# Pinning every product of the tensor engine in the order in which it is written, in a two-layer decoder trunk

## The chip, the cores and the metric

The kernel runs on one core of one Trainium2 chip, as one program and one launch. Its time is the device time of one execution in microseconds (us). A profiled execution gives the trace that is read below; its span runs from the first to the last instruction.

## The reference

The trunk has two layers over 256 tokens of 1024 features, all in float32. A layer normalises the stream, multiplies it with one wide matrix `w_in`, feeds the pieces to a gated short convolution and to a four-head retention, merges both with sigmoid gates, projects, and adds; then comes a squared-ReLU MLP of width 4096:

```python
def hybrid_layer(x, positions, ...):
    h = rmsnorm(x, norm_mix)
    proj = h @ w_in
    cb, cc, cu, q, k, v, g, ga, gb = jnp.split(proj, split_points, axis=-1)
    y_conv = short_conv_mixer(cb, cc, cu, conv_w, w_conv_out)
    y_ret = retention_mixer(q, k, v, g, positions, ret_norm, w_ret_out)
    merged = jax.nn.sigmoid(ga) * y_conv + jax.nn.sigmoid(gb) * y_ret
    x = x + merged @ w_o
    h2 = rmsnorm(x, norm_mlp)
    return x + jnp.square(jax.nn.relu(h2 @ w_up)) @ w_down
```

After the second layer a last RMSNorm is applied.

## The kernel before

**Data.** Features lie on the 128 partitions, in eight feature tiles k = 0 to 7, and tokens along the free dimension. The weights come in blocks of 1 MB (1024 inputs by 256 outputs), 152 in all, each loaded by one DMA into a `raw` tile (the first three in pieces). A float32 number is represented by two reduced-precision parts: ScalarE (ACT) rounds it to the high part (L99), VectorE (DVE) subtracts to get the low part (L100). This `split` is done to every weight block, in two halves, into a `parts` tile, and to every activation that is to be multiplied. There are three `raw` and three `parts` buffers.

**A block's products.** `proj` (L159) multiplies one block with an activation: for each of the eight feature tiles and both halves of the outputs one product of 512 columns (high weights with both activation parts) and one of 256 columns (low weights with the high part), so 32 products per block, all through the helper `mm` (L156, L157), all adding into one `ps` tile. Four products belong to each feature tile. There are three `ps` buffers, so up to three projections can be open at once. `collect` (L206) then copies one half of the tile on ACT and adds the other on DVE. The first `v` block of layer 0 is multiplied unsplit.

**Stages.** In each layer: four `v` blocks; the convolution's `cc`, `cu`, `cb`; `q`, `k`, `g`, `ga`, `gb`, with the retention's products set in between by `later`; then four blocks with `yc` (the convolution's output), four with `yr` (the retention's), four with `mg` (the merge), sixteen up blocks on `mlp` (the second norm's input) and sixteen down blocks on `up0` to `up3`. The merged tiles 2p and 2p+1 of `mg` are made by a chain behind the p-th `yr` block: copy, add, gate, add, split. The tiles of `mlp` are made behind the p-th `mg` block: two adds into the stream `x` (L578), then a scaling on ACT (L246) and its low part on DVE (L247). The next layer's norm input `mix` is made in the same way behind the down blocks (L614, L246, L247). The last two feature tiles of layer 1's down projection go through `proj_one`, which adds the residual by two products with an identity matrix.

**Norms.** The factor of a norm is applied after the products, so it may come late. Squares are taken on ACT (L254), added on GpSimd (POOL, L258) and folded (L267), split into `mix_sh` and `mix_sl` (or `mlp_sh`, `mlp_sl`), and summed over the partitions by two products with a matrix of ones, `column_sums` (L229), into `mix_st` (`mlp_st`). `later(n, ...)` writes such a piece behind the n-th block from there: layer 0's first sums are written behind the third `v` block.

**What sets the order.** The kernel is built with a scheduler that lays out each engine's instructions by its own model of times. It may exchange instructions on one engine where no data forbids it. An instruction that is handed to `tc.keep_in_program_order` keeps its place in the written order among those that are handed to it. Before, that holds for the first product of each column sum (L231) and for the first squares. Once built, every engine's order is fixed.

Of the kernel before, what the change touches and what calls it, by code (L numbers as in the profile page):

```python
# [48 lines left out]
def trunk_kernel(ctx, tc, px, pos, w, cst, mask, out):  # L49
    nc = tc.nc  # L50
# [19 lines left out]
    ones = const.tile([P, P], F32R, name="ones")  # L70
# [7 lines left out]
    def stile(name):  # L78
        return s8.tile([P, KT, T], F32, tag="s8", name=name)
# [50 lines left out]
    def whole_tokens(xs):  # L130

        ps = ps_main.tile([P, 2, 2, T], F32, tag="mm", name="ps")
        raw = next_block()
        for k in range(KT):
            for j in range(2):
                mm(ps[:, j, 0], xs[:, k, j * P:(j + 1) * P], raw[:, 2 * k:2 * k + 2, :], k == 0, k == KT - 1)
        run_waiting()
        t = t2("sum", "sum", 4)
        nc.scalar.copy(t, ps[:, :, 0, :])
        return t  # L140
# [13 lines left out]
            due[0][1](*due[0][2])  # L154

    def mm(o, a, b, start, stop):  # L156
        nc.tensor.matmul(o, lhsT=a, rhs=b, start=start, stop=stop, skip_group_check=True)  # L157

    def proj(act, n_blocks=1):  # L159

        ps = ps_main.tile([P, 2, 2, T], F32, tag="mm", name="ps")
        for b in range(n_blocks):
            blk = next_block()
            for k in range(KT):
                a = act[b].at(k)
                for j in range(2):
                    first, end = b == 0 and k == 0, b == n_blocks - 1 and k == KT - 1  # L170
                    mm(ps[:, j], blk[:, 0, 2 * k + j, :], a, first, False)
                    mm(ps[:, j, 1], blk[:, 1, 2 * k + j, :], a[:, 0], False, end)
            run_waiting()
        return ps
# [53 lines left out]

    def column_sums(o, hi, lo):  # L229

        tc.keep_in_program_order(nc.tensor.matmul(o, lhsT=ones, rhs=hi, start=True, stop=False))  # L231
        nc.tensor.matmul(o, lhsT=ones, rhs=lo, start=False, stop=True)

    class Norm:

# [35 lines left out]
        def total(self):  # L271

            st = ps_misc.tile([P, T], F32, tag="misc", name=f"{self.name}_st")
            column_sums(st, *self.sums)
            return st
# [80 lines left out]
    for layer in range(DEPTH):  # L356
# [125 lines left out]
        def head_sums(i):  # L482

            st = ps_misc.tile([P, 2, T], F32, tag="misc", name="var_ps")
            h = slice(2 * i, 2 * i + 2)
            column_sums(st, osq[:, 0, h, :], osq[:, 1, h, :])
            nc.vector.tensor_scalar(
                out=rm[:, 1, h, :], in0=st, scalar1=1.0 / T, scalar2=EPS, op0=ALU.mult, op1=ALU.add
            )
            nc.scalar.activation(rm[:, 0, h, :], st, AF.Sqrt, scale=1.0 / T, bias=eps)  # L490
# [130 lines left out]
    o = stile("o")  # L621
# [35 lines left out]
    m, r, a = (small.tile([P, 2], F32, tag=n, name=n) for n in ("fin_m", "fin_r", "fin_a"))  # L657
# [95 lines left out]
```

## Time and profile before

| | us |
|---|---|
| median of 3 runs | 891.73 |
| lowest, highest | 891.69, 893.56 |
| the profiled execution | 892.27 |
| its span | 890.1 |
| PE busy in it | 877.3 |
| DVE busy in it | 695.9 |
| ACT busy in it | 505.4 |
| POOL busy in it | 251.7 |

The profile gives for each engine when an instruction started, how long it took, and what ended the idle time before it. PE is TensorE; PEld is its loading of weights, which overlaps its products. The ends of products are modelled, so a product's own duration is longer than the distance to the next one: distances between starts are the better measure. The granted clock of TensorE over the span is 0.994 of full speed.

### The profile page before, as it was taken

What the parts mean: (1) busy time and instruction counts of PE and PEld (TensorE: products, weight loads), DVE (VectorE), ACT (ScalarE), POOL (GpSimd) and SP (SyncE); (2) the same over time, 40 slices, a digit from 0 to 9 for tenths busy, and PEclk for the clock granted to TensorE, in tenths of its full rate; (3) what the DMA queues carried; (4) which work ended last, traced back from release to release, by engine and by line L of the source; (5) the groups of instructions that cost most, each with busy time, mean ns of one, the idle gap of its engine ahead of it and who ended that gap; (6) DMA issues with size and microseconds to landing.
All of it is one profiled execution on the core that took longest, in us unless ns stands there. A gap on an engine that the chain in (4) does not pass through costs nothing.

```text
span 890.1 us, 12685 instructions
## 1 busy us (share of the span) xinstructions
PE 877.3 (99%) x5090; PEld 767.9 (86%) x5090; DVE 695.9 (78%) x785; ACT 505.4 (57%) x700; POOL 251.7 (28%) x170
## 2 busy tenths in 40 slices
PE   8999999999999999999999999999999999999996
PEld 6878888888888888888888888888888888888896
DVE  5989999799977966555588989998996897664451
ACT  6445636675556877444455554566654597764440
POOL 2883353421003322000046324443200323210110
PEclk9999999999999999999999999999999999999998
DMA  9645645444654655555545553555355555555521
GB/s 319 233 141 190 205 159 199 179 159 148 231 188 143 237 193 188 192 192 188 193 179 190 189 190 142 189 190 177 130 215 189 189 180 206 189 200 190 191 75 48
DMA packets 24682, 163.00 MB, mean 183 GB/s; under 512 B 2864, under 2 KB 3504, under 8 KB 5552
## 3 DMA queue, kind: packets, MB, share of 16 engines
q1 hardware_dynamic: 24336, 161.68, 51.3%
q8 instruction: 40, 0.66, 0.3%
q10 hardware_dynamic: 288, 0.52, 0.2%
q14 instruction: 18, 0.15, 0.0%
HBM read 161.14 MB, written 1.05 MB: 182 GB/s over the span
## 4 chain that ended last, share of the span: by engine, by line
PE 92%; POOL 3%; DVE 2%; DMA 1%; ACT 1%; issue 0%; SPq 0%; DVEq 0%; POOLq 0%; ACTq 0%
PE ps L157 89%; PE o_ps L157 1%; DVE parts L100 1%; POOL sum L412 1%; DMA raw<-w 1%; PE sc_ps L157 1%; DMA px_sb<-px 0%; ACT parts L99 0%; POOL v L412 0%; POOL mix_sum L258 0%; POOL red L333 0%; POOL sum L432 0%; DVE o L675 0%; POOL turns L339 0%; DVE rs_a L215 0%
## 5 line engine op out<-in xcount | busy, mean ns | idle before, releaser
L100 DVE TENSOR_TENSOR parts<-raw,parts 128x1024 fp32r<-128x1024 f32 (+1 forms) x304 | 411.2, 1384 | 70.4 <-ACT parts L99 69.5
L99 ACT CAST parts<-raw 128x1024 fp32r<-128x1024 f32 (+1 forms) x304 | 302.4, 1044 | 109.2 <-PE ps L157 78.1
L157 PE MATMUL ps<-mix,parts 128*128 128x512 f32 (+1 forms) x1792 | 323.0, 341 | 2.5 <-DVE parts L100 2.5
L157 PEld LDWEIGHTS ps<-mix,parts 128*128 128x128 f32 x1792 | 275.9, 189 | 44.0 <-DVE parts L100 2.8
L157 PE MATMUL ps<-up,parts 128*128 128x512 f32 (+1 forms) x1088 | 179.4, 326 | 0.0
L157 PE MATMUL ps<-mlp,parts 128*128 128x256 f32 (+1 forms) x1024 | 178.5, 335 | 0.0
L157 PEld LDWEIGHTS ps<-up,parts 128*128 128x128 f32 x1088 | 159.1, 188 | 19.6
L157 PEld LDWEIGHTS ps<-mlp,parts 128*128 128x128 f32 x1024 | 155.4, 188 | 22.4 <-issue 0.4
L210 DVE TENSOR_TENSOR sum<-ps,sum 128x512 f32<-128x512 f32 x87 | 59.4, 683 | 43.7 <-ACT sum L209 43.7
L209 ACT COPY sum<-ps 128x512 f32<-128x512 f32 x87 | 50.6, 582 | 75.2 <-PE ps L157 75.2
L594 POOL TENSOR_TENSOR u<-u,rr2m 128x512 f32<-128x512 f32 x32 | 47.7, 1492 | 123.4 <-ACT u L604 106.1
L258 POOL TENSOR_TENSOR mix_sum<-mix_sum,sq 128x512 f32<-128x512 f32 x8 | 12.6, 1574 | 145.1 <-ACT sq L254 145.1
L258 POOL TENSOR_TENSOR mlp_sum<-mlp_sum,sq 128x512 f32<-128x512 f32 x6 | 12.9, 2158 | 122.7 <-ACT sq L254 122.7
L157 PE MATMUL ps<-yr,parts 128*128 128x512 f32 (+1 forms) x256 | 44.7, 336 | 0.0
L157 PE MATMUL ps<-mg,parts 128*128 128x512 f32 (+1 forms) x256 | 44.7, 336 | 0.0
L157 PE MATMUL ps<-yc,parts 128*128 128x512 f32 (+1 forms) x256 | 44.7, 336 | 0.0
L157 PEld LDWEIGHTS ps<-yc,parts 128*128 128x128 f32 x256 | 39.1, 188 | 5.2
L157 PEld LDWEIGHTS ps<-yr,parts 128*128 128x128 f32 x256 | 39.1, 188 | 5.2
L157 PEld LDWEIGHTS ps<-mg,parts 128*128 128x128 f32 x256 | 39.1, 188 | 5.2
L157 PE MATMUL ps<-parts,mix 128*128 128x512 f32 (+1 forms) x224 | 39.8, 338 | 0.0
L157 PEld LDWEIGHTS ps<-parts,mix 128*128 128x128 f32 x224 | 34.2, 188 | 5.0
L100 DVE TENSOR_TENSOR up<-u,up 128x512 fp32r<-128x512 f32 x32 | 26.1, 820 | 0.0
(175 smaller groups left out, 666.6 us busy)
## 6 DMA issues: line engine op xcount, KB each, us to landing
raw<-w SPq DMA_DIRECT2D x149, 1024.0 KB, 4.8
raw<-w SPq DMA_DIRECT2D x3, 512.0 KB, 7.5
raw<-w SPq DMA_DIRECT2D x5, 256.0 KB, 6.1
px_sb<-px SPq DMA_DIRECT2D x3, 256.0 KB, 4.6
mask_sb<-mask SPq DMA_DIRECT2D x1, 512.0 KB, 7.2
out<-o SPq DMA_DIRECT2D x2, 256.0 KB, 2.3
out<-o ACTq DMA_DIRECT2D x2, 256.0 KB, 2.5
raw<-w SPq DMA_DIRECT2D x2, 128.0 KB, 2.7
```

Of the source, the lines that this page charges most:

```text
L99: nc.scalar.copy(hi, src)
L100: nc.vector.tensor_tensor(out=lo, in0=src, in1=hi.bitcast(F32), op=ALU.subtract)
L157: nc.tensor.matmul(o, lhsT=a, rhs=b, start=start, stop=stop, skip_group_check=True)
L209: nc.scalar.copy(t, ps[:, :, 1, :])
L210: nc.vector.tensor_tensor(out=t, in0=ps[:, :, 0, :], in1=t, op=ALU.add)
L258: nc.gpsimd.tensor_tensor(out=self.sum, in0=self.sum, in1=sq, op=ALU.add)
L412: nc.gpsimd.tensor_scalar(out=o_, in0=t[:, c, :], scalar1=mu[:, c:c + 1], scalar2=None, op0=ALU.subtract)
L594: nc.gpsimd.tensor_tensor(out=u, in0=u, in1=both(rr2), op=ALU.mult)
```

## The change

`mm` hands its product to `tc.keep_in_program_order`, and `column_sums` goes through `mm`. So all products of the layers keep the order in which the source writes them; the six warm-up products, the sums of the last norm and its broadcast do not go through `mm`.

```diff
     def mm(o, a, b, start, stop):
-        nc.tensor.matmul(o, lhsT=a, rhs=b, start=start, stop=stop, skip_group_check=True)
+        tc.keep_in_program_order(nc.tensor.matmul(o, lhsT=a, rhs=b, start=start, stop=stop, skip_group_check=True))
...
     def column_sums(o, hi, lo):
 
-        tc.keep_in_program_order(nc.tensor.matmul(o, lhsT=ones, rhs=hi, start=True, stop=False))
-        nc.tensor.matmul(o, lhsT=ones, rhs=lo, start=False, stop=True)
+        mm(o, ones, hi, True, False)
+        mm(o, ones, lo, False, True)
```

On PE at the start of layer 0, - being the order before and + the order now (`ps_268`, `ps_335` and `ps_409` are the third, fourth and fifth block's results, `mix0_st` the first norm's column sums):

```order
 L157 MATMUL ps_268<-parts_108,mix01_103 128x512
 L157 MATMUL ps_268<-parts_108,mix01_103 128x256
+L157 MATMUL mix0_st_308<-mix0_sh_254,ones_91 128x256
+L157 MATMUL mix0_st_308<-mix0_sl_255,ones_91 128x256
 L157 MATMUL ps_335<-parts_215,mix00_102 128x512
 L157 MATMUL ps_335<-parts_215,mix00_102 128x256
...
-L231 MATMUL mix0_st_308<-mix0_sh_254,ones_91 128x256
...
-L232 MATMUL mix0_st_308<-mix0_sl_255,ones_91 128x256
```

Both sums moved from inside the fifth block to a place in front of the fourth. The orders of POOL, ACT and DVE up to the instruction that writes `mix0_sl` are the same in both; behind it DVE's Newton steps for the norm's factor moved forward, in front of the splits of the seventh block.

On PE at the first `mg` block of layer 0 (`ps_2239` and `ps_2286` are the first and second `mg` projection, `mg0` holds feature tiles 0 to 3 and `mg1` tiles 4 to 7):

```order
 L157 MATMUL ps_2239<-mg0_2042,parts_2142 128x512
 L157 MATMUL ps_2239<-mg0_2042,parts_2142 128x256
-L157 MATMUL ps_2286<-mg0_2042,parts_2190 128x512
-L157 MATMUL ps_2286<-mg0_2042,parts_2190 128x256
...
+L157 MATMUL ps_2239<-mg1_2043,parts_2142 128x512
+L157 MATMUL ps_2239<-mg1_2043,parts_2142 128x256
```

Before, the first projection's 16 products on `mg0` were followed by 6 of the second, then came 8 on `mg1` (tiles 4 and 5), 10 and 8 of the second, 6 of the third, and only then the first's last 8 (tiles 6 and 7): 54 products stood in front of them. Now 24 do. At `mlp` three projections' 48 products on tiles 0 to 3 stood in front of the first on tiles 4 and 5; now 16 do, and the column sums stand behind the second block instead of the middle of the third. At layer 1's first block 35 stood in front of tile 6; now 24 do. Layer 1's `mg` and `mlp` have the same exchange. In the tail the two identity products stand behind 48 products of their projection, without ten of the next one in front of or between them.

On DVE between `mg` and `mlp` of layer 0, before (`px_sb` holds the stream, `mlp00` feature tiles 0 to 3 and `mlp01` tiles 4 to 7 of the norm's input):

```order
L578 SCALAR_TENSOR_TENSOR px_sb_88<-ps_2335,px_sb_88 128x512
L578 SCALAR_TENSOR_TENSOR px_sb_88<-ps_2384,px_sb_88 128x512
L100 TENSOR_TENSOR parts_2443<-raw_2442,parts_2443 128x1024 x2
L578 SCALAR_TENSOR_TENSOR px_sb_88<-ps_2384,px_sb_88 128x512
L247 SCALAR_TENSOR_TENSOR mlp01_2238<-px_sb_88,mlp01_2238 128x256 x4
L100 TENSOR_TENSOR mlp0_sl_2435<-mlp0_sum_2236,mlp0_sh_2434 128x256
```

and now:

```order
L578 SCALAR_TENSOR_TENSOR px_sb_88<-ps_2335,px_sb_88 128x512 x2
L100 TENSOR_TENSOR parts_2386<-raw_2385,parts_2386 128x1024 x2
L247 SCALAR_TENSOR_TENSOR mlp01_2238<-px_sb_88,mlp01_2238 128x256 x2
L578 SCALAR_TENSOR_TENSOR px_sb_88<-ps_2384,px_sb_88 128x512 x2
L100 TENSOR_TENSOR parts_2443<-raw_2442,parts_2443 128x1024 x2
L247 SCALAR_TENSOR_TENSOR mlp01_2238<-px_sb_88,mlp01_2238 128x256 x2
L100 TENSOR_TENSOR mlp0_sl_2435<-mlp0_sum_2236,mlp0_sh_2434 128x256
```

The adds of each `mg` projection now stand together, followed by one block's splits and that projection's two feature tiles, which is the sequence that the down projections have before and after. The order of the DMA queue is the same.

## Rows read from the trace of the kernel before

**Rows 1.** The page's first part: busy us, share of the span, instructions.
```profile
PE 877.3 (99%) x5090; PEld 767.9 (86%) x5090; DVE 695.9 (78%) x785; ACT 505.4 (57%) x700; POOL 251.7 (28%) x170
```

**Rows 2.** PE's waits, longest first: total us, times, longest us.
```profile
PE ps L157 <- DVE parts L100: 2.5, 1, 2.5
PE ps L157 <- DMA raw<-w: 1.2, 2, 0.9
```

**Rows 3.** The chain that ended last: start us, us, what.
```profile
64.78 2.21 DVE parts L100
67.04 63.75 PE ps L157 x351
...
150.08 5.65 PE ps L157 x32
...
714.61 154.39 PE ps L157 x924
```

**Rows 4.** Stretches around 67 us: length, busy us, PEclk, DMA share, GB/s.
```profile
31.55:67.00 35.45, 33.03 (x188) 28.40 (x186) 32.32 (x45) 16.47 (x23) 30.78 (x26) 1.00 0.51 178
64.58:67.04 2.46, 0.01 (x2) 0.01 (x1) 2.46 (x3) 0.00 (x0) 1.32 (x1) 1.00 0.00 0
67.04:70.50 3.46, 3.46 (x11) 2.98 (x12) 2.77 (x4) 1.75 (x3) 0.00 (x0) 0.51 0.37 107
70.50:74.00 3.50, 3.50 (x22) 3.03 (x21) 3.36 (x3) 2.00 (x4) 2.37 (x1) 1.00 0.48 201
```

**Rows 5.** PE in order of time, 13 to 33 us: start us, us, instruction.
```profile
13.22 17.00 PE L157 MATMUL ps<-parts,mix 128*128 128x512 f32 x96
30.06 1.08 PE L157 MATMUL ps<-mix,parts 128*128 128x512 f32 x5
...
32.27 0.28 PE L232 MATMUL mix_st<-mix_sl,ones 128*128 128x256 f32 x1
```

**Rows 6.** POOL in order of time, 26 to 30 us.
```profile
26.96 1.30 POOL L258 TENSOR_TENSOR mix_sum<-mix_sum,sq 128x512 f32<-128x512 f32 x1
28.34 1.60 POOL L267 TENSOR_TENSOR mix_sum<-mix_sum 128x256 f32<-128x256 f32 x1
```

**Rows 7.** DVE in order of time, 23 to 32 us.
```profile
23.03 2.35 DVE L100 TENSOR_TENSOR parts<-raw,parts 128x1024 fp32r<-128x1024 f32 x2
...
31.55 0.41 DVE L100 TENSOR_TENSOR mix_sl<-mix_sum,mix_sh 128x256 fp32r<-128x256 f32 x1
```

**Rows 8.** PE in order of time, the `mg` stage of layer 0 and of layer 1.
```profile
244.88 22.35 PE L157 MATMUL ps<-mg,parts 128*128 128x512 f32 x128
...
678.00 22.35 PE L157 MATMUL ps<-mg,parts 128*128 128x512 f32 x128
```

**Rows 9.** DVE, the last split of `mg` in layer 0 and in layer 1.
```profile
249.90 0.68 DVE L100 TENSOR_TENSOR mg<-m,mg 128x512 fp32r<-128x512 f32 x1
...
683.03 0.68 DVE L100 TENSOR_TENSOR mg<-m,mg 128x512 fp32r<-128x512 f32 x1
```

**Rows 10.** DVE at the start of layer 1.
```profile
448.75 2.39 DVE L247 SCALAR_TENSOR_TENSOR mix<-px_sb,mix 128x256 fp32r<-128x256 f32 x2
451.33 0.43 DVE L100 TENSOR_TENSOR mix_sl<-mix_sum,mix_sh 128x256 fp32r<-128x256 f32 x1 [0.19 <-ACT mix_sh L99]
```

**Rows 11.** PE at the start of layer 1.
```profile
444.95 11.33 PE L157 MATMUL ps<-parts,mix 128*128 128x512 f32 x64
456.12 0.28 PE L231 MATMUL mix_st<-mix_sh,ones 128*128 128x256 f32 x1
```

**Rows 12.** POOL at the start of layer 1.
```profile
448.62 1.36 POOL L258 TENSOR_TENSOR mix_sum<-mix_sum,sq 128x512 f32<-128x512 f32 x1 [20.82 <-ACT sq L254]
```

**Rows 13.** Line L247: count, shortest, median and longest ns, first and last start.
```profile
L247 DVE SCALAR_TENSOR_TENSOR mlp<-px_sb,mlp x16: 470/476/1519, 262.9 to 707.2; 128x256 fp32r<-128x256 f32 x16
```

**Rows 14.** PE in the tail, the first identity product.
```profile
862.36 0.28 PE L157 MATMUL ps<-x_parts,ident 128*128 128x256 f32 x1
```

**Rows 15.** DVE in the tail, the identity product's operand.
```profile
859.82 1.52 DVE L100 TENSOR_TENSOR x_parts<-px_sb,x_parts 128x256 fp32r<-128x256 f32 x1
```

## The prediction

> **What bounds the kernel now.** I read the busy times first: TensorE (PE) is busy 99% of the span, VectorE (DVE) 78% [rows 1]. A busy share alone does not say which engine is the bound, so PE's own waits come next, longest first: one of 2.46 us on a DVE split of a weight block, and two on the first loads, 1.2 us together [rows 2]. The chain of waits says the same: from 67.04 us to 869 us it is PE products, one stretch behind the other [rows 3]. In there PE waits for nothing, so whatever idle time the change puts in is added to the end. Before 67 us there is the one wait to be won, and what follows it: in the 3.46 us behind it the granted clock is 0.51 of full speed, that is the lower of the two levels (1.2 instead of 2.4 GHz), and it is full again afterwards [rows 4]. That costs 3.46 x 0.49 = 1.7 us more.
>
> **What the change does.** It adds and removes no instruction, and the order of the DMA queue stays as it was. On PE it moves products at seven places: the first norm's two column sums, `yr` to `mg` and `mg` to `mlp` in each layer (the `mlp` column sums among them), the down projection to layer 1's first blocks, and the identity products of the tail. At each of them the scheduler had put products of the next `ps` tiles in front of products whose operand is late. A pinned product waits instead, and all that is queued behind it on PE waits too. So for each place I compare when the operand is ready with when PE, without gaps, would come to it.
>
> *The first column sums.* Before, they stand inside the fifth block's products, the second one at 32.27 us [rows 5]. Pinned, they stand in front of the fourth block. 96 products take from 13.22 to 30.06 us, 0.1754 us each [rows 5], so the 64 of the second and third block end at 13.22 + 64 x 0.1754 = 24.45 us. What the sums read is late for reasons that the change does not touch: POOL's third add of squares is queued behind two subtractions that wait for the second block's mean, and runs from 26.96 us, and the fold from 28.34 to 29.94 us [rows 6]; ACT then rounds it, and DVE writes the low part from 31.55 to 31.96 us [rows 7]. The rows of POOL, ACT and DVE up to there stand in the same order in the changed kernel. With 0.05 us to be seen by PE (a split that ended at 64.78 + 2.21 = 66.99 let PE go on at 67.04 [rows 3]) and 0.12 us for the second sum (256 columns, a third of the 768 of two products at 0.35 us), the fourth block starts at 32.12 instead of 24.45 us: **+7.67 us**. The two sums' 2 x 0.12 us inside the fifth block are gone: **-0.23**.
>
> *The wait at 64.58 us.* DVE is 32.3 us busy between 31.55 and 67.00 [rows 4], and that work ends with the block that PE waits for. PE now comes to that block 7.4 us later, at about 72 us, so DVE has some 40 us for 32.3 us of work, and the Newton steps for the norm's factor now stand in front of the seventh block's splits, in time that PE leaves open. The wait goes: **-2.46 us**. Should every DVE step move back with PE's releases, it stays; that is the other end, 0. The slow clock behind it goes too (-1.7), but PE stands idle three times as long at 24.45 us, and I charge the same 1.7 us there (bounds 0 and 3.4, twice the one stretch that the trace shows). Net nothing.
>
> *`yr` to `mg`, twice.* PE's `mg` products begin at 244.88 us [rows 8]. The first pinned projection wants feature tile 6 after 24 products, each 0.1765 us (5.65 us for 32 in the chain [rows 3]): 244.88 + 24 x 0.1765 = 249.12 us. The DVE operation that writes tiles 6 and 7 runs from 249.90 to 250.58 us, at the end of a row of operations that keeps its order [rows 9]. Plus 0.05: PE waits 1.51 us. Before, these products came 54 places behind the start, at 254.4 us, and waited for nothing. In layer 1 the same two rows lie 5.71 us apart (678.00 to 683.71) against 5.70 here [rows 8, 9], so **+3.0 us** for two. One DVE operation of that row, 0.7 us, earlier or later in each is the uncertainty: 1.6 to 4.4.
>
> *`mg` to `mlp`, twice, and down to layer 1's `mix`, once.* The third shows its price already. DVE reads the last down block in two adds, splits a weight block, and then writes feature tiles 6 and 7 of the norm's input, which end at 448.75 + 2.39 = 451.14 us [rows 10]. PE begins layer 1's products at 444.95 us [rows 11] and, pinned, wants tile 7 after 28 products, at 449.89. It waits 451.19 - 449.89 = 1.30 us in all, in two pieces, since tile 6 is late too. At `mlp` DVE and ACT now have the same sequence (two adds, a block's splits, two splits of the norm's input), where before the adds of several projections came in a bunch; I take 1.30 for each. The lower end is 0: the two last splits took 2.39 us with POOL adding squares beside them [rows 12]; at their shortest, 0.47 us each [rows 13], they end at 449.7, in time. **+3.9 us** for three.
>
> *Nothing.* The tail's identity products now come 48 instead of 54 products behind that block's start. The first is at 862.36 us before [rows 14], six products of 0.118 us earlier is 861.65; its operand is ready at 859.82 + 1.52 = 861.34 us [rows 15]. Layer 1's column sums wait for nothing either: their low part is there at 451.76, their place at 456.12 us [rows 10, 11], and `mlp`'s now have that place too.
>
> **Sum:** 7.67 - 0.23 - 2.46 + 3.0 + 3.9 = +11.9 us on the profiled execution's 892.27 us (span 890.1 and 2.2 around it), which is 904.2. The median of the runs is 0.54 us below that execution: 903.6 us.
>
> **The rivals.**
> *The clock falls at the short waits too.* The trace has a fall after 2.46 us of idling [rows 4] and none at the start after 0.9 us [rows 2]; 1.3 to 1.5 us lie between. Each fall would cost 1.7 us, five of them 8.5: 905.3 to 912.1 us. Against it: all five are nearer to the 0.9 than to the 2.46, and three come in two pieces. The Trainium skill ("TensorE: Matmul & The Clock Gate", section "A second HAM failure mode: psum-queue depth-cycling") tells of a kernel whose short idle times between groups of products made the clock swing between its levels; by that rule the sum would be the 912. No row here shows it for a wait of this length.
> *DVE does not catch up:* the 2.46 us wait and its slow clock come back, 903.6 + 4.2 = 907.8 us. For it: DVE is the fullest engine beside PE in that stretch, and the convolution's chain through POOL stands in front of the split. Against it: about 8 us of spare time.
> *The last splits are in time:* DVE finds POOL quiet at the three transitions into `mlp` and `mix`: 903.6 - 3.9 = 899.7 us. Against it: ACT hands the squares to POOL at the same place of its order as in the row that I read.
> *The engine passes a waiting product.* If PE goes on with later products whose operands are there, the order in which they are written holds nothing up, and the 2.46 us with their 1.7 may be won: 887.6 to 891.7 us, not slower. It is decided at 24.45 us: the fourth block's splits run from 23.03 to 25.38 [rows 7], so an engine that can pass has 32 products to go on with. The one long wait of the trace does not settle it, because it does not show that any later block was ready. The Trainium skill (same page, section "Step-by-step: what each phase is for") says that only weight loads are pulled ahead and the matmuls stay in program order; by that rule this rival falls and the sum stays.
>
> **How the numbers follow.** Forecast 0.63; clock at some or all of the short waits 0.18; DVE does not catch up 0.08; splits in time 0.08; engine passes 0.03. The forecast by itself is 901 to 906 us. The range takes in the splits in time (899.7), DVE's wait (907.8) and up to three falls of the clock (908.7): 899.5 to 909. Outside are more falls and the last rival, about 0.12. A change of under 0.2% (1.8 us) cannot be told from none; only the last rival reaches there: slower 0.96, within 0.02, faster 0.02.
>
> **What would show it.** PE's waits: one of about 7.5 us on `mix_sl` near 24 us; one of 1.5 us on `mg` and one or two of 0.4 to 1.3 us on `mlp` or `mix` at each transition; none near 70 us on a weight block. The granted clock under full speed once, behind the long wait. I am wrong in the first term if PE's wait at 24 us is under 6 us, in the third if no wait names `mg`, in the clock if it falls behind a short wait, and altogether if PE's products at these places start in another order than the written one.

## The result, and the profile after

| | us | ratio to the kernel before |
|---|---|---|
| before, median of 4 runs beside it | 891.94 (891.69 to 893.56) | |
| changed, median of 4 runs | 900.2 (899.81 to 905.52) | 1.0103, 95% interval 1.0063 to 1.0142 |
| changed, another 4 runs later | 901.76 (900.87 to 903.67) | 1.0112, 1.0098 to 1.0126 |
| the profiled execution, changed | 900.0, its span 898.1 | |

The change makes the kernel about 1% slower: 8.3 us by the first four runs and 9.8 by the later four (891.96 us before, beside them), where the forecast was 11.9. The page's first part, columns as in [rows 1]:

```profile
PE 875.4 (97%) x5090; PEld 768.1 (86%) x5090; DVE 699.4 (78%) x785; ACT 507.3 (56%) x700; POOL 241.8 (27%) x170
```

The span is 8.0 us longer, and PE is not busy longer in it (875.4 against 877.3): PE stands idle for 10 us more and does the same work in 2 us less. PE's waits, which answer to [rows 2], name the places (total us, times, longest us):

```profile
PE mix_st L157 <- ACT mix_sh L99: 5.6, 1, 5.6
PE ps L157 <- DVE mg L100: 2.9, 2, 1.4
PE ps L157 <- DVE mlp L247: 2.0, 2, 1.0
...
PE mix_st L157 <- DVE mix_sl L100: 1.0, 1, 1.0
PE ps L157 <- DVE mix L247: 0.8, 1, 0.8
```

The wait of 2.5 us on a weight block's `parts` is gone, and there are six new ones: one on the column sums' operand in two pieces (`mix_sh`, `mix_sl`), two on `mg`, two on `mlp`, one on `mix`. PE in order of time at these places (start us, us, instruction, in brackets the idle time before it and what ended it) answers to [rows 5, 8 and 11]:

```profile
13.12 11.59 PE L157 MATMUL ps<-parts,mix 128*128 128x512 f32 x64
30.34 0.58 PE L157 MATMUL mix_st<-mix_sh,ones 128*128 128x256 f32 x1 [5.63 <-ACT mix_sh L99]
31.91 0.58 PE L157 MATMUL mix_st<-mix_sl,ones 128*128 128x256 f32 x1 [1.00 <-DVE mix_sl L100]
32.30 7.30 PE L157 MATMUL ps<-parts,mix 128*128 128x512 f32 x32
...
247.54 4.32 PE L157 MATMUL ps<-mg,parts 128*128 128x512 f32 x24
253.31 5.01 PE L157 MATMUL ps<-mg,parts 128*128 128x512 f32 x27 [1.44 <-DVE mg L100]
...
271.44 4.33 PE L157 MATMUL ps<-mlp,parts 128*128 128x512 f32 x24
276.79 7.49 PE L157 MATMUL ps<-mlp,parts 128*128 128x512 f32 x40 [1.02 <-DVE mlp L247]
284.12 0.28 PE L157 MATMUL mlp_st<-mlp_sh,ones 128*128 128x256 f32 x1
...
450.75 4.56 PE L157 MATMUL ps<-parts,mix 128*128 128x512 f32 x25
456.11 7.25 PE L157 MATMUL ps<-parts,mix 128*128 128x256 f32 x39 [0.80 <-DVE mix L247]
463.20 0.28 PE L157 MATMUL mix_st<-mix_sh,ones 128*128 128x256 f32 x1
```

Read the starts, not the bracket: a bracket leaves out the modelled end of the product before. The fourth block starts at 32.30 instead of some 24.5 us, 7.8 later. From 247.54 to 253.31 are 5.77 us for 24 products that take 24 x 0.1733 = 4.16: 1.61 us on `mg`. From 271.44 to 284.12 are 12.68 us for 64 products that take 11.1 to 11.3: about 1.5 on `mlp`; in the same way about 1.4 in layer 1 and, from 450.75 to 463.20, about 1.3 on `mix`. The five are 7.4 us.

The granted clock behind the long wait and around two of the short ones (length, busy us by engine, PEclk, DMA share, GB/s), which answers to [rows 4]:

```profile
32.30:36.00 3.70, 3.70 (x14) 3.18 (x14) 3.67 (x7) 0.00 (x0) 3.53 (x3) 0.53 0.68 263
36.00:40.00 4.00, 4.00 (x25) 3.53 (x24) 3.21 (x7) 0.77 (x2) 3.74 (x6) 1.00 0.75 262
245.00:255.00 10.00, 8.56 (x49) 7.33 (x48) 7.56 (x10) 3.73 (x5) 0.00 (x0) 1.00 0.47 166
270.00:280.00 10.00, 8.98 (x51) 7.46 (x50) 8.65 (x10) 5.07 (x8) 3.01 (x3) 1.00 0.61 210
```

The clock is at its lower level behind the long wait only: 3.7 x 0.47 = 1.7 us.

So the steps of the sum are there, and add to more than the difference: 7.8 + 1.7 + 7.4, less the 2.46 and 1.7 us of [rows 4] that went, and less 0.2 for the sums inside the fifth block, is 12.5, and the span is 8.0 longer. Some 4.5 us came back elsewhere. Most of them are in the chain of waits (start us, us, what), in stretches in which PE waits for nothing. Before, in layer 1's first stage:

```profile
456.51 107.41 PE ps L157 x608
```

The same products, and those around layer 0's scores (the retention's products of `q` and `k`, `sc_ps`), after:

```profile
32.50 101.39 PE ps L157 x576
...
134.47 5.55 PE ps L157 x32
...
463.59 105.39 PE ps L157 x608
```

608 products take 2.02 us less, 173.3 ns each instead of 176.7, at the full granted clock in both. In layer 0, 32 products between two scores take 5.55 instead of the 5.65 of [rows 3]; the 576 in front of them are 99.8 us at 173.3 ns and 1.6 of low clock. At 176.7 ns they would take 1.9 us more. So PE's stream has two spacings, and in each layer's first stage it is in another one than before: 1.9 us, 0.4 between layer 0's scores and 2.0 in layer 1. I did not know of them when I made the forecast: its 0.1765 us per product came from rows at one of them.

The rest is small. Layer 1's `mg` products ran at 176.7 ns behind their wait and lost 0.4 us; and 0.45 us came back at PE's last wait, at which the granted clock fell in the kernel before and did not fall now. Before, then after:

```profile
882.77 1.16 PE L669 MATMUL rb<-spread,fin_r 128*128 128x128 f32 x4 [1.20 <-DVE fin_r L666]
```

```profile
891.22 0.71 PE L669 MATMUL rb<-spread,fin_r 128*128 128x128 f32 x4 [1.20 <-DVE fin_r L666]
```

Place by place, the changed kernel's PE is 3.1 us behind at layer 0's first score (133.73 against 130.63 us), 5.1 at layer 1's (568.82 against 563.75), 8.45 at these last products, and the span is 8.0 longer.

### The profile page after: what moved, and what is told of

The parts are those of the page before. It is cut to its first block, busy times and chain, and to the rows that moved or that the text cites. A ratio compares the mean times of both kernels' runs of the same rounds, so it can differ in the third digit from the quotient of the medians.

```text
span 898.1 us, 12681 instructions
## 1 busy us (share of the span) xinstructions
PE 875.4 (97%) x5090; PEld 768.1 (86%) x5090; DVE 699.4 (78%) x785; ACT 507.3 (56%) x700; POOL 241.8 (27%) x170
## 4 chain that ended last, share of the span: by engine, by line
PE 93%; DVE 3%; DMA 1%; POOL 1%; issue 1%; ACT 1%; SPq 0%; DVEq 0%; POOLq 0%; ACTq 0%
PE ps L157 90%; DVE parts L100 2%; PE o_ps L157 1%; DMA raw<-w 1%; PE sc_ps L157 1%; DMA px_sb<-px 0%; POOL sum L412 0%; ACT parts L99 0%; DVE mlp L247 0%; POOL mix_sum L258 0%; DVE sum L210 0%; DVE o L675 0%; PE var_ps L157 0%; DVE px_sb L578 0%; DVE mix L247 0%
## 5 line engine op out<-in xcount | busy, mean ns | idle before, releaser
L157 PE MATMUL ps<-mix,parts 128*128 128x512 f32 (+1 forms) x1792 | 317.0, 338 | 0.0
L157 PE MATMUL ps<-mlp,parts 128*128 128x512 f32 (+1 forms) x1024 | 179.2, 336 | 2.0 <-DVE mlp L247 2.0
L594 POOL TENSOR_TENSOR u<-u,rr2m 128x512 f32<-128x512 f32 x32 | 49.5, 1549 | 131.5 <-ACT u L604 111.4
L258 POOL TENSOR_TENSOR mix_sum<-mix_sum,sq 128x512 f32<-128x512 f32 x8 | 12.5, 1566 | 145.1 <-ACT sq L254 145.1
L157 PE MATMUL ps<-parts,mix 128*128 128x512 f32 x224 | 42.0, 348 | 0.8 <-DVE mix L247 0.8
L258 POOL TENSOR_TENSOR mlp_sum<-mlp_sum,sq 128x512 f32<-128x512 f32 x6 | 8.0, 1332 | 124.2 <-ACT sq L254 124.2
```

Of the source, the lines that this page charges most:

```text
L157: tc.keep_in_program_order(nc.tensor.matmul(o, lhsT=a, rhs=b, start=start, stop=stop, skip_group_check=True))
L258: nc.gpsimd.tensor_tensor(out=self.sum, in0=self.sum, in1=sq, op=ALU.add)
L594: nc.gpsimd.tensor_tensor(out=u, in0=u, in1=both(rr2), op=ALU.mult)
```

## The experiments

Two questions were open: what the long wait really costs, and whether the two spacings are the missing 4 us and what sets them. A joint is a place where one stage's products begin to read what the stage before has just made: `yr` to `mg`, `mg` to `mlp`, and the down projection to layer 1's `mix`. All times are medians, with the lowest and highest run in round brackets and the 95% interval of a ratio in square ones; "before" is 891.9 to 892.0 us in every comparison.

**The sums later.** Layer 0's column sums are written, and pinned, behind the fifth block.

```diff
-        later(3 if layer == 0 else 2, factors)
+        later(5 if layer == 0 else 2, factors)
```

> The changed kernel with one number changed: layer 0's column sums are written, and so pinned, behind the fifth block of the queries instead of the third. Theory of the waits (the time comes from PE standing in front of operands that are late): the sums' operand, ready at about 31.9 us, is wanted at 13.1 + 128 x 0.176 = 35.6 us, so the wait of 6.6 us in the changed kernel's trace goes, and the slow clock behind it (1.7 us) goes with it; the convolution's work on DVE no longer has that cover, so the wait near 64 us with its own slow clock may come back (0 to 4.2 us). That gives 900.0 - 8.0 - 1.7 = 890.3 us, up to 894.5. The six other waits stay as they are. Theory of the two spacings (the stream of products runs at 173.3 or at 176.7 ns per product, and pinning decides which after the sums): the time that goes from the sums on is decided by which spacing the trace shows behind them; 176.7 up to the scores would add 2 us, 892.3 to 896.5. Rival: the long wait is not on the path, because DVE would have been late at the next block anyway; then the time stays within 2 us of 900.

Measured: 898.52 us (897.1 to 899.68), ratio 1.0070 [1.0055, 1.0085]. The rival is right: the long wait went, and only 1.7 us with it (0.3 between the profiled executions). PE's waits in this kernel:

```profile
...
PE sc_ps L157 <- ACT k_parts L99: 2.7, 1, 2.7
PE ps L157 <- DVE parts L100: 2.4, 2, 1.4
...
PE sc_ps L157 <- DVE k_parts L100: 0.5, 1, 0.5
```

Two waits on weight blocks (at 65 and 78 us) and one on the scores' operand `k_parts` (at 128 us) have come. By the distances between starts they cost 1.2, 1.7 and 5.4 us, with the low clock behind the last, 8.3 in all. DVE has the same work up to there in both kernels (91.6 us busy from 33 to 131 us, 91.4 in the changed kernel): without the long wait PE only comes to it sooner, and waits later.

**The same with less work for DVE.** In layer 0 the convolution's 16 multiply-adds are left out, once from the kernel above and once from the changed kernel.

```diff
+                if layer == 0:
+                    continue
                 nc.vector.scalar_tensor_tensor(
                     out=acc[:, j, 1:], ...
```

> The kernel with the late column sums, and in layer 0 the convolution's 16 multiply-adds on DVE (lines 438 and 441) left out, 0.47 us each by its trace, 7.5 us of DVE before the scores; the convolution's other operations stay. Theory that DVE sets when layer 0's first stage ends (PE must lose about 8 us to it somewhere, and the long wait at 24 us in the changed kernel only took that place): without this work the waits at 78 us (1.5 us with what stands around it) and at the scores (5.1 us) go, and the one at 65 us, ahead of most of it, stays: 898.5 - 6.6 = 892, at most 2 us away by the spacing of layer 0's products. Rival, that the late sums cost the time through their own order (the factor's chain comes too late for the rotations): the waits on k_parts stay at about 5 us and the time at 897 or above.

> The changed kernel with the same 16 multiply-adds of DVE left out in layer 0. Theory that the long wait for the column sums leaves DVE enough time: PE has no wait on DVE between 32 us and the mg products in the changed kernel, so the time stays at 900, or moves by the 2 us per layer of the products' spacing. Rival, that DVE's load slows PE in that stage without a wait (ports or memory shared): the spacing of the products falls below 173.3 ns and the time by more than 2 us.

Measured: with the sums late 891.99 us (890.99 to 896.56), 6.5 less than with that work; with the sums as changed 901.03 (899.71 to 903.41), nothing gained. Both as the first theory says. With the sums late, the waits on `k_parts` are gone from PE's list, and one on a weight block stays:

```profile
PE ps L157 <- DVE mg L100: 2.9, 2, 1.4
...
PE ps L157 <- DVE parts L100: 1.0, 1, 1.0
```

So up to layer 0's scores DVE is as much the bound as PE, and some of the idle time that the pinned sums cost PE is idle time that PE would have had later. In the kernel before, DVE's share of such a stretch says the same (columns as in [rows 4], the third busy time is DVE's):

```profile
80.00:120.00 40.00, 40.00 (x228) 34.68 (x227) 39.84 (x42) 22.45 (x31) 17.36 (x10) 1.00 0.61 210
```

**The joints free.** `mm` pins no product of the `mg` projections, of the first three up blocks and of layer 1's first two `v` blocks; all others stay pinned.

```diff
+    pinned = [True]
     def mm(o, a, b, start, stop):
-        tc.keep_in_program_order(nc.tensor.matmul(...))
+        ins = nc.tensor.matmul(...)
+        if pinned[0]:
+            tc.keep_in_program_order(ins)
...
+            pinned[0] = False
             ps = proj([mg])
+            pinned[0] = True
```

> The changed kernel with the pin taken off at the joints alone: all mg projections, the first three blocks of the mlp's up projection and the first two of layer 1's values are left to the scheduler, which puts them in the same places as in the kernel before; the first column sums stay pinned in front of the fourth block. Theory of the waits: the five waits of 0.8 to 1.45 us (two on mg, two on mlp, one on mix) go, with their second pieces 2 x 1.6 + 1.48 + 1.44 + 1.27 = 7.4 us: 892.6 us, and PE's waits name neither mg nor mlp nor mix. Theory of the two spacings: layer 1's first stage, whose interleaved products are back, goes to 176.7 ns per product as in the kernel before, 600 x 3.4 ns = 2.0 us more: 894.6 us. Rival: what is won at a joint is lost at the next block, because DVE and ACT are no sooner done with its splits; then other waits take their place and the time stays at 897 or above.

Measured: 896.31 us (894.52 to 897.58), ratio 1.0044 [1.0029, 1.0059]; the profiled execution 897.58. No wait names `mg`, `mlp` or `mix` (that for the column sums in layer 0 stays), and all 128 `mg` products take the 22.35 us of [rows 8] again. Between the profiled executions the time falls by 2.4 us and not by 7.4, and the trace shows why: both first stages run at 176.7 ns. The chain:

```profile
32.48 104.28 PE ps L159 x576
...
462.54 107.41 PE ps L159 x608
```

The 576 products take 2.9 us more than in the changed kernel's trace, 1.9 by the spacing and 1.0 because behind the same long wait the clock stayed at its lower level for 5.7 us here instead of 3.7. With 0.4 between the scores and 2.0 in layer 1 that is 5.3, and 7.4 less 5.3 is 2.1. The median falls by 3.9 us; which spacings the other three runs had is not shown.

**Both edits.** 

> Both edits of the two kernels beside it: the sums behind the fifth block, and the joints free. PE's order then differs from the kernel before only at the first column sums (as an adjacent pair between two blocks, where before they stood one by one inside the fifth block) and at the tail's identity products. Theory of the waits alone: it comes out at the time before, 891.7, less 0 to 4.2 us if the wait near 64 us does not come back. Theory of the two spacings: where the adjacent pair of sums leaves the stream at 173.3 ns per product, layer 0's first stage gains 600 x 3.4 ns = 2.0 us, so 885.5 to 889.7; where it goes to 176.7, as before, 887.5 to 891.7. Rival: the two edits do not add up, because without the long wait DVE falls behind by as much; then 894 or above.

Measured: 893.84 us (892.05 to 895.09), ratio 1.0018 [1.0009, 1.0028]. Below the rival's bound by a hair and above every other number: the savings of the two edits do add up (900.2 - 1.7 - 3.9 = 894.6), but the first one is the small saving that was measured for it, and my numbers took the large one. PE waits for DVE in layer 0 again, 2.3 us on weight blocks and 2.1 on `k_parts`.

**Products that nothing reads.** The changed kernel, with extra products between up blocks.

```diff
+            for cols in PROBES[layer].get(p, ()):
+                extra = ps_misc.tile([P, 2, T], F32, tag="misc", name="probe")
+                rhs = norm.act.at(0) if cols == 512 else norm.act.at(0)[:, 0, :cols]
+                mm(extra if cols == 512 else extra[:, 0, :cols], ones, rhs, True, True)
```

> The changed kernel with 16 more products that nothing reads (ones times the norm's input, 128, 256 or 512 columns wide), put between blocks of the mlp's up projection, one, two or three in a row, at six places in each layer; the outputs are not touched. They cost about 2 us by themselves. Theory that an interruption of the stream sets its spacing: behind some of these places the mean spacing changes between 173.3 and 176.7 ns and stays so up to the next place, depending on the width and number of the products put in. Rival, that the spacing belongs to the stage (what DVE, ACT, POOL and the DMA do beside it): the spacing stays as in the changed kernel's trace, 173.3 ns nearly throughout this stage, whatever is put in.

Measured: one execution, 907.83 us. The chain in layer 0's up projection; each stretch is two blocks, between two insertions:

```profile
298.11 0.12 PE probe L161
298.22 11.10 PE ps L161 x64
309.32 0.12 PE probe L161
309.44 11.31 PE ps L161 x64
320.75 0.23 PE probe L161 x2
320.98 11.10 PE ps L161 x64
```

64 products take 11.10 us, or 11.31 with 176.7 ns each, and change from one to the other only where something was put in. So the spacing does not belong to the stage: DVE, ACT, POOL and the DMA have the same work beside each of these blocks. But no rule by width or number held: one product of 256 columns changed it at 309 us and not at 298 us.

**Switching it in the kernel before.** One such product in each layer's first stage, and, in another kernel, one in each layer's fifth up block.

```diff
+            if (name, n) in ((("cc", 3),) if layer == 0 else (("cc", 1),)):
+                probe(act[0])
             ps = proj(act)
```

> The kernel before with two more products that nothing reads (ones times the norm's input, 256 columns, 0.12 us each): one ahead of the eleventh weight block in layer 0, at about 78 us, one ahead of the eighth in layer 1, at about 475 us; nothing else moves on any engine. In the kernel before the stream runs at 176.7 ns per product at both places. Theory that an interruption sets the spacing: it goes to 173.3 ns behind each, 290 products up to the scores in layer 0 (1.0 us, up to 1.6 if it stays through the scores), 520 in layer 1 (1.8 us), less 0.24: 892.0 - 2.6 = 889.4, between 888.5 and 890. Rival, that the spacing belongs to the stage or to the place where the first products of the layer were put: it stays at 176.7 and the time is 892.2.

> The counterpart: the kernel before with the same product put into each layer's up projection, one product behind the start of the fifth block, where the stream runs at 173.3 ns per product up to the end of the down projection (about 870 products in layer 0, 780 in layer 1). Theory that an interruption sets the spacing: it goes to 176.7 ns, 3.0 and 2.7 us, plus 0.24: 892.0 + 5.9 = 897.9; if only one of the two places switches, 895. Rival, that the spacing belongs to the stage: 892.2.

Measured: 891.93 us (ratio 1.0003 [0.9994, 1.0012]) for the first, no gain, and 895.79 (1.0043 [1.0029, 1.0056]) for the second. The first missed twice. In layer 1 the product at 484 us changed nothing, the stream stayed at 176.7. In layer 0 the stream ran at 173.3 already behind the wait at 65 us, and PE came a microsecond earlier to the scores, to wait there:

```profile
129.64 0.50 PE L157 MATMUL sc_ps<-q_parts,k_parts 128*128 128x256 f32 x2
130.62 0.39 PE L157 MATMUL sc_ps<-q_parts,k_parts 128*128 128x256 f32 x1 [0.48 <-DVE k_parts L100]
```

Behind these scores it goes on at 130.98 instead of 131.13 us: 0.15 us earlier. That is DVE's bound again, seen from the other side. The second kernel's chain:

```profile
283.92 174.94 PE ps L157 x991
...
459.10 105.39 PE ps L157 x608
```

Behind the product at 284 us, 960 products run at 176.7 ns, and 780 in layer 1, 5.9 us with the products themselves as expected; what I had not expected is that layer 1's first stage then ran at 173.3 ns (105.39 us) and gave 2.1 us back: 897.9 - 2.1 = 895.8.

**Choosing how layer 1 is entered.** So one such product late in layer 0 might be enough, 0.12 us for 2. Two kernels, both the kernel before with one product late in layer 0's down projection. In the second it stands five products later, and so also between the two products of a pair. The edit of the first:

```diff
+            if layer == 0 and p == 3:
+                probe(ups[0])
             ps = proj(ups, 4)
```

> The kernel before with one more product that nothing reads (256 columns, 0.12 us), ahead of the last block of layer 0's down projection, at about 439 us. Nothing else moves. The theory that interruptions set the spacing says what happens there (173.3 to 176.7 ns, as behind each of the single products put into a 173.3 stretch so far), and it says that layer 1's column sums, entered in the other spacing, may leave the stream at 173.3 ns: in the kernel with the product at 284 us, layer 1 was entered at 176.7 ns and its first stage then ran at 173.3. Then 600 products and some of the scores' gain 2.0 to 2.3 us, less 0.12 and 60 x 3.4 ns = 0.2 at the end of the down projection: 891.9 - 1.8 = 890.1. If the sums leave it at 176.7 whatever comes in: 892.2. Which of the two depends, by the rows so far, on the place in the pattern that the sums meet, and that I can't work out.

> The same with the product five products later, between the two products of a pair. That is the place in the block, and the distance to layer 1 up to a multiple of six products, of the kernel in which layer 1's first stage ran at 173.3 ns. If the pattern repeats every six products, layer 1 is entered in the same place of it: first stage at 173.3 ns, 890.1 us. If the entry is left to chance, it may come out as in the kernel before, 892.2.

Measured: 892.54 us (1.0008 [0.9999, 1.0017]) and 890.11 us (0.9981 [0.9973, 0.9990]). The product stands at 422 and 423 us (not at 439, as I wrote). The chain of the first, then of the second:

```profile
422.14 0.12 PE probe L157
422.26 33.90 PE ps L157 x192
...
456.40 107.41 PE ps L157 x608
```

```profile
423.15 0.12 PE probe L157
423.27 32.90 PE ps L157 x187
...
456.41 105.39 PE ps L157 x608
```

Both switch the end of layer 0 to 176.7 ns, and both reach the column sums at the same time; but layer 1's first stage runs at 176.7 ns in the first and at 173.3 in the second. The order of all other products is the same, and the times are 2.4 us apart (eleven runs each, 891.85 to 894.5 and 889.17 to 891.95 us). It is not the sums that decide, as I had taken it to be: the second stream has changed before it comes to them. The last 18 products ahead of the sums, in the first kernel, then in the second:

```profile
452.87 3.18 PE ps L157 x18
```

```profile
452.93 3.12 PE ps L157 x18
```

By the starts in the trace the change comes at 451 us, where the scheduler has exchanged products of layer 1's first two blocks. The kernel with the product at 284 us changes there too, at 454 us, and so does the kernel before, the other way: it comes from 173.3 and leaves at 176.7 ns. In the four traces of kernels that have this exchange and come to it at 173.3 ns, layer 1's 608 products behind the sums take 107.4 us; in all six with these products pinned, where there is no exchange but the wait on `mix`, 105.4. So the 2.0 us of layer 1 come from the change itself: it takes an interruption away that had slowed the stream.

What the exchange does to a stream that comes at 176.7 ns depends on where the stream was cut before. The place of the second kernel, which I took from the kernel with the product at 284 us by counting in sixes, was the right one. That the pattern has six products fits these two kernels, and fits the starts, whose distances repeat every six products at 176.7 ns; a third place was not tried, and the count of five and the place inside a pair are not told apart. The second kernel is 0.2% faster than the kernel before.

**Once more.** 

> The changed kernel unchanged, once more: its stages behind a wait ran at 173.3 ns in one trace and at 176.7 in another of the same order. If each wait throws the stream into one of the two, the runs spread over about 2 us for each first stage and 0.4 us for the mg products: times between 899.5 and 905, and a profile whose spacings differ from the first one's at least in one stage that follows a wait. Rival, that the first trace's spacings belong to this order of products: the same spacings again, and runs within 1 us of 900.

Measured: 901.76 us (900.87 to 903.67). The spread came, but the profile answers only in part: both first stages at 173.3 ns again. Of the stages behind a wait, layer 0's `mg` products had changed, to 176.7 ns (0.4 us). The chain shows another part of the spread:

```profile
33.46 102.30 PE ps L157 x576
```

It begins 1 us later than in the first trace, since PE had waited 2.4 us for first loads instead of 1.2, and takes 0.9 us longer by the low clock. The kernel with the unread products, whose order is the same up to 298 us, had 103.07 us for these 576, at 176.7 ns. So one order gives either spacing behind a wait, and the 1.9 us of layer 0, unlike the 2.0 of layer 1, belong to the execution as much as to the order.

## Why the prediction was right, and where it was not

*The first column sums, +7.67.* The fourth block is 7.8 us later. Where the idle time comes from is as said: the operand is late for reasons that the change does not touch. The wait came in two pieces, since PE began the first sum as soon as the high part was there, and the second sum took 0.39 us at the lower clock instead of 0.12. PE did not go on with the fourth block, whose splits were done at 25.34 us, so the rival in which the engine passes a waiting product falls. (The Trainium skill's sentence that the matmuls stay in program order, "TensorE: Matmul & The Clock Gate", section "Step-by-step: what each phase is for", agrees with this 5.63 us wait.)

*The wait at 64.58 us, -2.46.* Gone, and DVE caught up. The two experiments on DVE's work show why this belongs together: DVE is the bound up to the scores, and the long wait gives it time that PE would otherwise have lost there. So pinning the sums in front of the fourth block costs only 1.7 us more than pinning them two blocks later, and not the whole term.

*The clock, netted to nothing.* 1.7 us behind the long wait, as charged, in the profiled execution; up to 2.9 in others (3.7 x 0.5 and 2 x 0.5 where the joints were free). No fall at any of the five joints, with waits of 0.8 to 1.5 us, in no trace of a kernel that has them pinned. The rule in the Trainium skill that spoke for such falls ("TensorE: Matmul & The Clock Gate", section "A second HAM failure mode: psum-queue depth-cycling") is not borne out at these joints. The prediction's reading of the trace left out one fall: at PE's last wait, 1.20 us, the clock fell in the kernel before. A short wait alone does not rule a fall out, then.

The 1.7 us taken for the fall at 67 us in the kernel before were too many as a price. In three kernels with the same order up to there (the product at 284 us, and the last pair) PE waits 1.9 to 2.4 us at this place, and the granted clock stays at 1.00. From the waits of the last one:

```profile
PE ps L157 <- DVE parts L100: 2.4, 1, 2.4
...
PE sc_ps L157 <- DVE k_parts L100: 0.5, 1, 0.5
```

PE comes to layer 0's scores 1.1 to 1.3 us earlier than in the kernel before (129.37 to 129.52 against 130.63 us), waits there for `k_parts`, and goes on behind the first scores only 0.3 to 0.4 us earlier (130.71 to 130.87 against 131.13). DVE takes the rest back.

*`yr` to `mg`, 1.51 each:* 1.61 each. Most of the difference is the spacing, 24 x 0.0032 us, since PE came to its operand at 173.3 and not 176.5 ns per product.

*`mg` to `mlp` and down to `mix`, 1.30 each:* 1.5, 1.4 and 1.3. The rival with the splits in time falls.

*Nothing:* the tail's identity products and layer 1's column sums wait for nothing.

*The sum, +11.9:* these terms measure 12.5, and the kernel became only 8.3 us slower (7.7 by the two profiled executions; 9.8 by the later four runs). The step that failed is one that I did not write down: that all products which wait for nothing keep their duration when their order changes. 1.9 us were won so in layer 0's first stage with 0.4 between its scores, and 2.0 in layer 1's. The kernel with the joints free brings the exchange at the start of layer 1 back, and 2.0 us with it; the last pair of kernels shows the same 2.0 us by themselves. In layer 0 the 173.3 ns are worth something only because PE, after its long wait, is behind DVE: in the kernel before they would have gained little, 0.15 us up to the first scores in the kernel with the product at 85 us. The forecast's time, 903.6, was 3.4 us too high for it. That the range held the time is in this part luck: its low end was there for splits in time, which did not come, and none of the rivals names the spacing.

What stays open: why the stream has these two spacings, and which of them a wait leaves it in. In its eight runs the changed kernel took 899.8 to 905.5 us; the spacing of its stages, the low clock's length and the first loads were seen to differ between its traces, but no trace shows an execution of 905 us.

## What to carry to other kernels

An order pinned as written makes the engine wait wherever the next product's operand is late, and the price can be worked out place by place from the rows of the kernel before, operand ready against place reached. But before such an idle time is charged in full, look whether another engine is the bound of the same stretch (here DVE, busy 39.84 of 40 us): then it only moves a wait. And a stretch without waits is not a constant: compare its time per product in two traces before and after, since 2% there over 600 products was a quarter of the effect. Both can meet at one place: at layer 1's start the exchange of products hid a wait of 1.3 us and left the stream slower by 2.0, so that the pinned kernel is 5.8 us behind at that layer's first product and 5.1 at its first score. A kernel with this place alone pinned was not run.

## What the runs showed of the hardware that was not expected

- A steady stream of products with their weight loads, pairs of 512 and 256 columns, runs at 173.3 or 176.7 ns per product at full granted clock (layer 1's 608 products behind the sums in 105.39 or 107.41 us in every trace that has no product put in there), and keeps the one it is in for hundreds of products. A product put in, an exchange of two projections' products, the column sums, or a wait can change it; a product of 256 columns did at 309 us and did not at 298 and 484 us.
- Which one follows the same interruption can depend on the place where the stream was cut long before: one product put in five products later, 28 us ahead of the exchange, made 2.4 us of the whole kernel's time.
- Behind the same wait for the column sums, 6.4 to 6.6 us, the clock stayed at its lower level for 3.7 us of PE's work in one execution and 5.7 in another. Behind the wait on a weight block at some 65 us it fell in the kernel before (2.46 us, then 0.51 for 3.46 us) and in the one with the product at 85 us (2.1 us), and did not in three others (1.9 to 2.4 us, 1.00). Behind waits of 0.8 to 1.5 us at the joints it never fell; at the wait of 1.20 us near the end it fell in three traces of thirteen, where four products then took 1.00 to 1.22 us instead of 0.71. So the length of the wait alone does not say whether it falls.
